# Matmul with rotary embedding: tiles in pairs of three PSUM banks, one VectorE multiply a pair, and every second tile transposed by VectorE blocks from four-piece loads

## The chip, the cores and the metric

One core of one Trainium2 chip. The metric is device microseconds (us) of one execution; lower is better. An execution more than 1.5% above the fastest of its kernel is called slow.

## The reference

```python
# x: 16 x 512 x 768 fp32, weight: 768 x 768 fp32, cos/sin: 512 x 64, 12 heads of 64
y = np.matmul(x, weight).reshape(batch, seq, n_heads, head_dim)
y1, y2 = y[..., :32], y[..., 32:]
out1 = y1 * cos1 - y2 * sin1
out2 = y2 * cos2 + y1 * sin2
out = np.concatenate([out1, out2], axis=-1).reshape(batch, seq, hidden)
```

There are 64 tiles of 128 rows. Both kernels cast each tile to fp16 and transpose it, so that the hidden dimension lies on the partitions, before they multiply it. In the kernel before that is 64 casts and, on TensorE, 384 transposes of 128 x 128, six a tile.

## The kernel before

A tile takes this way: a load of 384 KB on SyncE's queue; a cast to fp16 on ScalarE; six transposes on TensorE into `pt`, a copy out of PSUM on ScalarE; twelve matmuls into a two-bank PSUM tile `psy` (three such buffers); two multiplies on VectorE (by cos, and by the signed sin with the halves swapped); an add on GpSimd; a store on ScalarE's queue.

```python
    def load(i):
        xss[i] = xpool.tile([P, H], FP32, tag="xs", name="xs")
        nc.sync.dma_start(out=xss[i], in_=xv[i // SB, i % SB])
    ...
    def transpose(i, eng):
        xc = x16.pop(i)
        pt = pt_pool.tile([P, NKT, P], FP16, tag="pt", name="pt")
        for kt in range(NKT):
            nc.tensor.transpose(pt[:, kt, :], xc[:, ts(kt, P)], ident)
        xTT[i] = tpool.tile([P, NKT, P], FP16, tag="xT", name="xT")
        copy(eng, xTT[i], pt)
    ...
    def store(i):
        nc.scalar.dma_start(out=ov_dram[i // SB, i % SB], in_=ovs.pop(i))
    ...
    for i in range(FIRST, NMB):
        if i + AHEAD - FIRST < NMB:
            load(i + AHEAD - FIRST)
        if i + 1 < NMB:
            transpose(i + 1, nc.scalar)
        if 4 < i + 2 < NMB:
            cast(i + 2, nc.scalar)
        if i < NMB - 1:
            for kt in range(NKT):
                mm(i, kt)
            rope_whole(i)          # two multiplies on VectorE, one add on GpSimd
            store(i - 3)
```

## Time and profile before

| what | before |
|---|---|
| median of 3 runs (lowest to highest) | 166.97 us (166.83 to 168.94) |
| span of the profiled run, mean granted clock | 166.9 us, 0.983 |
| busy: TensorE, VectorE, GpSimd, ScalarE | 92%, 74%, 69%, 59% |

The table is read with the chain of waits in mind: TensorE is nearly full and is 88% of the chain, so a part counts if it shortens TensorE's stream and nothing else falls behind.

### The profile page before, as it was taken

How to read it: one execution, taken by the hardware profiler on the slowest of the kernel's cores; microseconds unless marked ns; L12 is line 12 of the kernel's file. 1: busy time of each engine (PE TensorE's matmuls, PEld its weight loads, DVE VectorE, ACT ScalarE, POOL GpSimd, SP SyncE). 2: the span in 40 equal slices, each digit the busy share in tenths (PEclk: the TensorE clock that was granted, in tenths of full speed). 3: DMA queues.
4: the chain of work that ended last, by engine and by line, in shares of the span. 5: the costliest groups of instructions: out<-in, count | busy, mean ns of one | idle time of the engine just before them, and what ended most of it. 6: DMA issues, size and time to landing. Idle time of an engine off the chain costs nothing.

```text
span 166.9 us, 3136 instructions
## 1 busy us (share of the span) xinstructions
PE 153.6 (92%) x1165; PEld 98.5 (59%) x1165; DVE 122.9 (74%) x142; ACT 97.9 (59%) x127; POOL 114.4 (69%) x67
## 2 busy tenths in 40 slices
PE   7657699999999999999999999999999999999930
PEld 2224466666666666666666666666666666666610
DVE  0522598777877688877778877778877778777792
ACT  3053366667766667766667766667666667666400
POOL 0000099777787777887777887777887777877770
PEclk9987999999999999999999999999999999999997
DMA  4999999999999999999999999999999984345544
GB/s 128 405 402 403 403 404 369 301 375 406 340 372 343 328 350 345 350 326 381 335 327 370 347 330 351 337 327 361 368 349 350 300 323 170 146 161 192 213 166 188
DMA packets 19887, 53.19 MB, mean 319 GB/s; under 512 B 2336, under 2 KB 2848, under 8 KB 19872
## 3 DMA queue, kind: packets, MB, share of 16 engines
q1 hardware_dynamic: 10368, 27.92, 49.5%
q10 hardware_dynamic: 9504, 25.07, 37.8%
q8 instruction: 9, 0.15, 0.5%
q14 instruction: 6, 0.05, 0.1%
HBM read 27.82 MB, written 25.17 MB: 317 GB/s over the span
## 4 chain that ended last, share of the span: by engine, by line
PE 88%; DMA 4%; ACT 2%; DVE 2%; issue 1%; SPq 1%; DVEq 0%
PE psy L103 74%; PE pt L93 13%; DMA xs<-in_x_dram 4%; PE psy L216 1%; DVE ov L130 1%; ACT xc L69 1%; ACT xT L69 1%; DVE qv L122 1%; SPq L80 1%; DVE tv L116 0%; SPq L75 0%; DVEq L130 0%; DVEq L116 0%
## 5 line engine op out<-in xcount | busy, mean ns | idle before, releaser
L130 POOL TENSOR_TENSOR ov<-tv,qv 128x768 f32<-128x768 f32 x63 | 114.2, 1816 | 47.4 <-DVE qv L122 46.2
L103 PE MATMUL psy<-w_sb,xT 128*128 128x512 f16 x756 | 135.1, 329 | 2.5 <-ACT xT L69 1.8
L103 PEld LDWEIGHTS <-xT 128*128 128x128 f16 x756 | 71.8, 99 | 44.9 <-ACT xT L69 2.1
L116 DVE TENSOR_TENSOR tv<-psy,cos_sb 128x768 f32<-128x768 f32 (+1 forms) x65 | 61.4, 944 | 31.7 <-PE psy L103 30.5
L69 ACT COPY xT<-pt 128x768 f16<-128x768 f16 x63 | 50.3, 798 | 51.2 <-PE pt L93 51.2
L122 DVE TENSOR_TENSOR qv<-psy,tee_sb 128x768 f32<-128x768 f32 (+1 forms) x65 | 60.7, 934 | 0.0
L69 ACT CAST xc<-xs 128x768 f16<-128x768 f32 x63 | 52.7, 836 | 5.8 <-DMA xs<-in_x_dram 5.8
L93 PE MATMUL pt<-ident,xc 128*128 128x128 f16 x384 | 31.9, 219 | 2.9 <-ACT xc L69 2.2
L93 PEld LDWEIGHTS <-xc 128*128 128x128 f16 x384 | 26.6, 98 | 12.3 <-ACT xc L69 3.0
L83 DVE CAST w_sb<-w_raw 128x768 f16<-128x768 f32 x6 | 3.3, 558 | 4.1 <-DMA w_raw<-in_weight_dram 4.1
L141 PE MATMUL cold_ps<-cold 128*128 128x512 f16 x13 | 4.6, 514 | 1.2 <-DVE cold L146 1.2
L141 PEld LDWEIGHTS <-cold 128*128 128x128 f16 x13 | 1.5, 126 | 3.3 <-issue 1.9
L71 DVE CAST xc<-xs 128x768 f16<-128x768 f32 x1 | 0.6, 560 | 3.7 <-DMA xs<-in_x_dram 3.7
L69 ACT ACT_TABLE_LOAD x1 | 1.3, 1283 | 2.1 <-issue 2.1
L216 PE MATMUL psy<-w_sb,xT 128*128 128x384 f16 x12 | 2.1, 326 | 0.0
L130 DVE TENSOR_TENSOR ov<-tv,qv 128x384 f32<-128x384 f32 x2 | 1.7, 862 | 0.1
L216 PEld LDWEIGHTS <-xT 128*128 128x128 f16 x12 | 1.2, 98 | 0.8
L71 DVE COPY xT<-pt 128x768 f16<-128x768 f16 x1 | 0.6, 556 | 0.6 <-PE pt L93 0.6
L146 DVE MEMSET cold<- 128x256 uint32 x1 | 0.3, 272 | 0.9 <-PEq L244 0.9
L244 POOL MEMSET const-float32-0.0<- 128x1 f32 x1 | 0.1, 98 | 0.2 <-issue 0.2
L185 DVE TENSOR_SCALAR tee_sb<-tee_sb 128x128 f32<-128x128 f32 x1 | 0.2, 220 | 0.0
L244 POOL MEMSET const-bfloat16-1.0<- 128x1 bf16 x1 | 0.1, 101 | 0.0
(2 smaller groups left out, 0.2 us busy)
## 6 DMA issues: line engine op xcount, KB each, us to landing
xs<-in_x_dram SPq DMA_DIRECT2D x64, 384.0 KB, 5.6
out_dram<-ov ACTq DMA_DIRECT2D x63, 384.0 KB, 4.8
w_raw<-in_weight_dram SPq DMA_DIRECT2D x6, 384.0 KB, 5.9
out_dram<-ov SPq DMA_DIRECT2D x2, 192.0 KB, 2.2
cos_sb<-in_cos_dram ACTq DMA_DIRECT2D x1, 128.0 KB, 5.2
tee_sb<-in_sin_dram ACTq DMA_DIRECT2D x1, 128.0 KB, 6.2
ident<-identity ACTq DMA_DIRECT2D x1, 32.0 KB, 3.6
```

The lines of the kernel that those rows point to most:

```text
L69: eng.copy(out=o, in_=i_)
L71: eng.tensor_copy(out=o, in_=i_)
L80: nc.sync.dma_start(out=w_raw[:, kt], in_=wv[:, kt])
L83: nc.vector.tensor_copy(out=w_sb[:, kt], in_=w_raw[:, kt])
L93: nc.tensor.transpose(pt[:, kt, :], xc[:, ts(kt, P)], ident)
L103: nc.tensor.matmul(psys[i][:, ds(noff, nsz)], xTT[i][:, kt, :], w_sb[:, kt, ds(noff % H, nsz)], start=(kt == 0), stop=(kt == NKT - 1),)
L116: nc.vector.tensor_tensor(out=tv.rearrange("p (h d) -> p h d", d=D), in0=ps.rearrange("p (h d) -> p h d", d=D), in1=cos_sb[:, sb, :].unsqu ...
L122: nc.vector.tensor_tensor(out=qv.rearrange("p (h t d) -> p h t d", t=2, d=HD), in0=ps.rearrange("p (h t d) -> p h t d", t=2, d=HD)[:, :, : ...
L130: add_eng.tensor_tensor(out=ov[:, ds(c0, n)], in0=tv, in1=qv, op=ADD)
L141: nc.tensor.matmul(cold_ps, cold[:, 0:P], cold, start=True, stop=True)
L146: nc.vector.memset(cold, 0.0)
L216: nc.tensor.matmul(psys[i][:, n, 0:sz], xTT[i][:, kt, :], w_sb[:, kt, ds(c0, sz)], start=(kt == 0), stop=(kt == NKT - 1),)
```

## The change

The intent is to take half of the transposes off TensorE. Tiles are handled in pairs, in a PSUM tile of three banks, so that one VectorE multiply (by cos and sin together, 3072 columns) and one GpSimd add (with the half swap, 1536 columns) serve a pair. From pair 3 on, the second tile of a pair is transposed by VectorE in blocks of 32 x 32. That completes a transpose only if the blocks lie in other places (with these tiles loaded whole, in experiment 1, the result has a relative error of 0.825). The load puts them there: four DMAs of 32 partitions each with runs of 768 B, two issued from SyncE and two from ScalarE. Pairs are also stored with one DMA instead of two, the loads at the start are reordered, and the last two pairs go tile by tile.

```diff
+    def by_blocks(n, s):
+        return n > 2 and s == 1
...
-    def load(i):
-        xss[i] = xpool.tile([P, H], FP32, tag="xs", name="xs")
-        nc.sync.dma_start(out=xss[i], in_=xv[i // SB, i % SB])
+    def load(n, s):
+        b, r = where(n, s)
+        xss[n, s] = xpool.tile([P, H], FP32, tag="xs", name="xs")
+        if by_blocks(n, s):
+            load_part(n, 0)
+            load_part(n, 1)
+        else:
+            nc.sync.dma_start(
+                out=xss[n, s], in_=x[b].rearrange("(p r) h -> r p h", r=SB)[r]
+            )
+
+    def load_part(n, q):
+        b, r = where(n, 1)
+        src = x[b].rearrange("(j a r) (q k) -> r q a j k", r=SB, a=R, q=NQ)   # R = 32, NQ = 4
+        dst = xss[n, 1].rearrange("p (j k) -> p j k", j=NQ)
+        eng = nc.sync if q < 2 else nc.scalar
+        eng.dma_start(out=dst[ts(q, R)], in_=src[r, q])
+
+    def load_rest(n):
+        if n < NP and by_blocks(n, 1):
+            load_part(n, 2)
+            load_part(n, 3)
...
+    def transpose_blocks(n, s):
+        xT = tpool.tile([P, NT, P, 2], FP16, tag="xT", name="xT")
+        nc.vector.transpose(
+            out=xT.bitcast(FP32).rearrange("p t m e -> p (t m e)"),
+            in_=x16.pop((n, s)).bitcast(FP32),
+        )
+        xTT[n, s] = xT.rearrange("p t m e -> p t e m")
...                                  # the loop over pairs
+        if n + 1 < NP and by_blocks(n + 1, 1):
+            transpose_blocks(n + 1, 1)
+        if n < NP - 1:
+            for c in CHUNKS:
+                mm(n, 0, *c)
...
+            prepare_b(n + 1, 0)      # ScalarE: copy of the transposed tile out of PSUM
+            prepare_a(n + 2, 0)      # ScalarE: cast
+            for c in CHUNKS:
+                mm(n, 1, *c)
...
+            prepare_a(n + 2, 1)      # ScalarE: cast
+            if n >= 3:
+                store(n - 3, nc.scalar)
+            load_rest(n + DEPTH - 2) # two more DMAs in ScalarE's stream
...
+                rope(n, 0, 2 * H, nc.gpsimd)
```

More of the change, by code (lines that the diff above doesn't have):

```diff
@@ L34, with where @@
     HD = D // 2
-    NKT = H // P
-    NMB = B * S // P
+    R = 32
+    NQ = P // R
+    NT = H // (2 * P)
     SB = S // P
-    NSPLIT = [(0, 512), (512, H - 512)]
-    HALVES = [(0, H // 2), (H // 2, H // 2)]
-    FIRST = 3
-    AHEAD = 8
-    xv = x.rearrange("b (p r) h -> b r p h", r=SB)
-    ov_dram = out.rearrange("b (p r) h -> b r p h", r=SB)
+    NP = B * SB // 2
+    CHUNKS = [(t, e) for t in range(NT) for e in range(2)]
+    DEPTH = 8
+    TAIL = 2
+    def where(n, s):
+        return 2 * (n // SB) + s, n % SB
+    def by_blocks(n, s):
+        return n > 2 and s == 1
     konst = ctx.enter_context(tc.tile_pool(name="konst", bufs=1))
     ident = konst.tile([P, P], FP16)
-    cos_sb = konst.tile([P, SB, D], FP32)
-    tee_sb = konst.tile([P, SB, D], FP32)
-    w_raw = konst.tile([P, NKT, H], FP32)
-    w_sb = konst.tile([P, NKT, H], FP16)
-    xpool = ctx.enter_context(tc.tile_pool(name="xpool", bufs=AHEAD + 3))
-    cpool = ctx.enter_context(tc.tile_pool(name="cpool", bufs=4))
-    tpool = ctx.enter_context(tc.tile_pool(name="tpool", bufs=FIRST + 2))
-    rpool = ctx.enter_context(tc.tile_pool(name="rpool", bufs=4))
-    opool = ctx.enter_context(tc.tile_pool(name="opool", bufs=5))
+    cold = konst.tile([P, 512], FP16)
+    sin_sb = konst.tile([P, SB, D], FP32)
+    csn = konst.tile([P, 2, SB, D], FP32)
+    w_raw = konst.tile([P, NT, 2, H], FP32)
+    w_sb = konst.tile([P, NT, 2, H], FP16)
+    xpool = ctx.enter_context(tc.tile_pool(name="xpool", bufs=2 * DEPTH + 2))
+    cpool = ctx.enter_context(tc.tile_pool(name="cpool", bufs=6))
+    tpool = ctx.enter_context(tc.tile_pool(name="tpool", bufs=7))
+    rpool = ctx.enter_context(tc.tile_pool(name="rpool", bufs=3))
+    opool = ctx.enter_context(tc.tile_pool(name="opool", bufs=4))
     pt_pool = ctx.enter_context(tc.tile_pool(name="pt", bufs=2, space=bass.MemoryType.PSUM))
-    py_pool = ctx.enter_context(tc.tile_pool(name="py", bufs=3, space=bass.MemoryType.PSUM))
-    cold = konst.tile([P, 512], FP16)
+    py_pool = ctx.enter_context(tc.tile_pool(name="py", bufs=2, space=bass.MemoryType.PSUM))
     cold_ps = pt_pool.tile([P, 512], FP32, tag="pt", name="cold_ps")
-    xss, x16, xTT, psys, ovs = {}, {}, {}, {}, {}
+    xss, x16, xTT, psys, tqs, ovs = {}, {}, {}, {}, {}, {}
     def copy(eng, o, i_):
@@ L71, in copy @@
             eng.tensor_copy(out=o, in_=i_)
-    def load(i):
-        xss[i] = xpool.tile([P, H], FP32, tag="xs", name="xs")
-        nc.sync.dma_start(out=xss[i], in_=xv[i // SB, i % SB])
-    wv = weight.rearrange("(kt p) n -> p kt n", p=P)
-    def load_w(kt):
-        nc.sync.dma_start(out=w_raw[:, kt], in_=wv[:, kt])
-    def cast_w(kt):
-        nc.vector.tensor_copy(out=w_sb[:, kt], in_=w_raw[:, kt])
-    def cast(i, eng):
-        x16[i] = cpool.tile([P, H], FP16, tag="xc", name="xc")
-        copy(eng, x16[i], xss.pop(i))
@@ L89, in transpose @@
-    def transpose(i, eng):
-        xc = x16.pop(i)
-        pt = pt_pool.tile([P, NKT, P], FP16, tag="pt", name="pt")
-        for kt in range(NKT):
-            nc.tensor.transpose(pt[:, kt, :], xc[:, ts(kt, P)], ident)
-        xTT[i] = tpool.tile([P, NKT, P], FP16, tag="xT", name="xT")
-        copy(eng, xTT[i], pt)
-    def mm(i, kt, parts=NSPLIT):
-        if i not in psys:
-            psys[i] = py_pool.tile([P, 2, 512], FP32, tag="psy", name="psy").rearrange(
+    def load(n, s):
[8 more added lines that the diff above has]
+            )
@@ new lines, in load_part, with load_w @@
+    def load_part(n, q):
[8 more added lines that the diff above has]
+            load_part(n, 3)
+    wv = weight.rearrange("(p t e) n -> t e p n", t=NT, e=2)
+    def load_w(t, e):
+        nc.sync.dma_start(out=w_raw[:, t, e], in_=wv[t, e])
@@ new lines, in cast_w, with cast, transpose @@
+    def cast_w(t, e):
+        nc.vector.tensor_copy(out=w_sb[:, t, e], in_=w_raw[:, t, e])
+    def cast(n, s, eng):
+        xc = cpool.tile([P, H], FP16, tag="xc", name="xc")
+        x16[n, s] = xc
+        src = xss.pop((n, s))
+        if by_blocks(n, s):
+            src = src.rearrange("p (j a t e) -> p t (j a) e", j=NQ, t=NT, e=2)
+        else:
+            src = src.rearrange("p (m t e) -> p t m e", t=NT, e=2)
+        copy(eng, xc.rearrange("p (t m e) -> p t m e", t=NT, e=2), src)
+    def transpose(n, s, eng):
+        xc = x16.pop((n, s)).rearrange("p (t m e) -> p t e m", t=NT, e=2)
+        pt = pt_pool.tile([P, NT, 2, P], FP16, tag="pt", name="pt")
+        for t, e in CHUNKS:
+            nc.tensor.transpose(pt[:, t, e, :], xc[:, t, e, :], ident)
+        xT = tpool.tile([P, NT, 2, P], FP16, tag="xT", name="xT")
+        copy(eng, xT, pt)
+        xTT[n, s] = xT
@@ new lines, in transpose_blocks, with alone, mm @@
+    def transpose_blocks(n, s):
[5 more added lines that the diff above has]
+        xTT[n, s] = xT.rearrange("p t m e -> p t e m")
+    def alone(n):
+        return n >= NP - 2
+    def mm(n, s, t, e, c0=0, c1=H):
+        key = (n, s) if alone(n) else n
+        base = 0 if alone(n) else s * H
+        if key not in psys:
+            psys[key] = py_pool.tile([P, 3, 512], FP32, tag="psy", name="psy").rearrange(
@@ L100, in mm @@
                 "p b n -> p (b n)"
             )
-        for noff, nsz in parts:
-            nc.tensor.matmul(
-                psys[i][:, ds(noff, nsz)],
-                xTT[i][:, kt, :],
-                w_sb[:, kt, ds(noff % H, nsz)],
-                start=(kt == 0),
-                stop=(kt == NKT - 1),
-            )
-    def rope(i, c0, n, ps, add_eng):
-        sb = i % SB
-        nh = n // D
-        tv = rpool.tile([P, H], FP32, tag="tv", name="tv")[:, :n]
-        qv = rpool.tile([P, H], FP32, tag="qv", name="qv")[:, :n]
+            if n < 2:
+                nc.tensor.matmul(
+                    psys[n][:, 512:1024], cold[:, 0:P], cold, start=True, stop=False
+                )
@@ new lines, in mm @@
+        cut = 256 if base else 512
+        for lo, hi in ((0, cut), (cut, H)):
+            lo, hi = max(lo, c0), min(hi, c1)
+            joined = n < 2 and 512 <= base + lo < 1024
+            if lo < hi:
+                nc.tensor.matmul(
+                    psys[key][:, ds(base + lo, hi - lo)],
+                    xTT[n, s][:, t, e, :],
+                    w_sb[:, t, e, ds(lo, hi - lo)],
+                    start=((t, e) == CHUNKS[0] and not joined),
+                    stop=((t, e) == CHUNKS[-1] and not (joined and s == 0)),
+                )
@@ L116, in rope @@
+    def rope(n, c0, c1, add_eng):
+        r = n % SB
+        w = c1 - c0
+        nh = w // D
+        if n not in tqs:
+            tqs[n] = rpool.tile([P, 2, 2 * H], FP32, tag="tq", name="tq")
+            ovs[n] = opool.tile([P, 2 * H], FP32, tag="ov", name="ov")
+        tq = tqs[n][:, :, ds(c0, w)]
+        ov = ovs[n][:, ds(c0, w)]
+        ps = psys[n, c0 // H][:, ds(c0 % H, w)] if alone(n) else psys[n][:, ds(c0, w)]
         nc.vector.tensor_tensor(
-            out=tv.rearrange("p (h d) -> p h d", d=D),
@@ L118, in rope @@
-            in0=ps.rearrange("p (h d) -> p h d", d=D),
-            in1=cos_sb[:, sb, :].unsqueeze(1).broadcast_to((P, nh, D)),
+            out=tq.rearrange("p j (h d) -> p j h d", d=D),
+            in0=ps.rearrange("p (h d) -> p h d", d=D)
+            .unsqueeze(1).broadcast_to((P, 2, nh, D)),
+            in1=csn[:, :, r, :].unsqueeze(2).broadcast_to((P, 2, nh, D)),
             op=MULT,
         )
-        nc.vector.tensor_tensor(
-            out=qv.rearrange("p (h t d) -> p h t d", t=2, d=HD),
-            in0=ps.rearrange("p (h t d) -> p h t d", t=2, d=HD)[:, :, ::-1, :],
-            in1=tee_sb[:, sb, :].rearrange("p (t d) -> p t d", t=2)
-            .unsqueeze(1).broadcast_to((P, nh, 2, HD)),
-            op=MULT,
-        )
@@ L129, in rope @@
-        ov = ovs[i]
-        add_eng.tensor_tensor(out=ov[:, ds(c0, n)], in0=tv, in1=qv, op=ADD)
-    def rope_whole(i):
-        ovs[i] = opool.tile([P, H], FP32, tag="ov", name="ov")
-        rope(i, 0, H, psys.pop(i)[:, 0:H], nc.gpsimd)
-    def store(i):
-        nc.scalar.dma_start(out=ov_dram[i // SB, i % SB], in_=ovs.pop(i))
-    def warm(n):
-        for _ in range(n):
+        add_eng.tensor_tensor(
+            out=ov.rearrange("p (h t d) -> p h t d", t=2, d=HD),
+            in0=tq[:, 0].rearrange("p (h t d) -> p h t d", t=2, d=HD),
+            in1=tq[:, 1].rearrange("p (h t d) -> p h t d", t=2, d=HD)[:, :, ::-1, :],
+            op=ADD,
+        )
@@ L141, in warm, with store @@
+    def store(n, eng, c0=0, c1=2 * H):
+        b, r = where(n, 0)
+        dst = out.rearrange("b (p r) h -> r p b h", r=SB)[r, :, b : b + 2]
+        src = ovs[n].rearrange("p (b h) -> p b h", b=2)
+        if c1 - c0 < 2 * H:
+            s = c0 // H
+            dst = dst[:, s, c0 - s * H : c1 - s * H]
+            src = src[:, s, c0 - s * H : c1 - s * H]
+        eng.dma_start(out=dst, in_=src)
+    def warm(k):
+        for _ in range(k):
             nc.tensor.matmul(cold_ps, cold[:, 0:P], cold, start=True, stop=True)
@@ L147 @@
     nc.scalar.dma_start(out=ident, in_=id_dram.ap())
-    load(0)
-    load_w(0)
-    load_w(1)
-    load(1)
-    nc.scalar.dma_start(out=cos_sb, in_=cos.rearrange("(p r) d -> p r d", r=SB))
-    nc.scalar.dma_start(out=tee_sb, in_=sin.rearrange("(p r) d -> p r d", r=SB))
-    load_w(2)
-    load_w(3)
-    load(2)
-    load_w(4)
-    load_w(5)
-    for i in range(FIRST, AHEAD):
-        load(i)
-    warm(9)
-    cast(0, nc.vector)
-    transpose(0, nc.vector)
-    warm(4)
-    for kt in (0, 1):
-        cast_w(kt)
-        mm(0, kt)
@@ L169 @@
-    cast(1, nc.scalar)
-    transpose(1, nc.scalar)
-    mm(1, 0)
-    mm(1, 1)
-    for kt in (2, 3):
-        cast_w(kt)
-        mm(0, kt)
-        mm(1, kt)
-    cast(2, nc.scalar)
-    transpose(2, nc.scalar)
-    for kt in range(4):
-        mm(2, kt)
-    cast_w(4)
-    for i in range(FIRST):
-        mm(i, 4)
-    cast_w(5)
+    for n in (0, 1):
+        for s in (0, 1):
+            load(n, s)
+    for t, e in CHUNKS:
+        load_w(t, e)
+    load(2, 0)
+    nc.sync.dma_start(out=csn[:, 0], in_=cos.rearrange("(p r) d -> p r d", r=SB))
@@ new lines, with prepare_a, prepare_b @@
+    nc.sync.dma_start(out=sin_sb, in_=sin.rearrange("(p r) d -> p r d", r=SB))
+    load(2, 1)
+    for n in range(3, DEPTH):
+        for s in (0, 1):
+            load(n, s)
+    def prepare_a(n, s):
+        if n < NP:
+            cast(n, s, nc.scalar)
+    def prepare_b(n, s):
+        if n < NP and not by_blocks(n, s):
+            transpose(n, s, nc.scalar)
+    warm(10)
+    cast(0, 0, nc.vector)
+    transpose(0, 0, nc.vector)
+    cast(0, 1, nc.scalar)
+    warm(4)
+    transpose(0, 1, nc.scalar)
@@ L185 @@
+    cast(1, 0, nc.vector)
+    warm(4)
+    transpose(1, 0, nc.vector)
+    cast(1, 1, nc.scalar)
+    warm(4)
+    transpose(1, 1, nc.scalar)
+    for k, c in enumerate(CHUNKS):
+        cast_w(*c)
+        mm(0, 0, *c)
+        mm(0, 1, *c)
+        if k > 0:
+            mm(1, 0, *CHUNKS[k - 1])
+    nc.vector.tensor_copy(out=csn[:, 1, :, 0:HD], in_=sin_sb[:, :, HD:D])
     nc.vector.tensor_scalar_mul(
-        out=tee_sb[:, :, 0:HD], in0=tee_sb[:, :, 0:HD], scalar1=-1.0
+        out=csn[:, 1, :, HD:D], in0=sin_sb[:, :, 0:HD], scalar1=-1.0
@@ L187 @@
     )
-    cast(3, nc.scalar)
-    mm(0, 5)
-    rope_whole(0)
-    mm(1, 5)
-    rope_whole(1)
-    transpose(3, nc.scalar)
-    cast(4, nc.scalar)
-    mm(2, 5)
-    rope_whole(2)
-    for i in range(FIRST, NMB):
-        if i + AHEAD - FIRST < NMB:
-            load(i + AHEAD - FIRST)
-        if i + 1 < NMB:
-            transpose(i + 1, nc.scalar)
-        if 4 < i + 2 < NMB:
-            cast(i + 2, nc.scalar)
-        if i < NMB - 1:
-            for kt in range(NKT):
-                mm(i, kt)
-            rope_whole(i)
-            store(i - 3)
@@ L210 @@
-    i = NMB - 1
-    ovs[i] = opool.tile([P, H], FP32, tag="ov", name="ov")
-    for n, (c0, sz) in enumerate(HALVES):
-        for kt in range(NKT):
-            if i not in psys:
-                psys[i] = py_pool.tile([P, 2, 512], FP32, tag="psy", name="psy")
-            nc.tensor.matmul(
-                psys[i][:, n, 0:sz],
-                xTT[i][:, kt, :],
-                w_sb[:, kt, ds(c0, sz)],
-                start=(kt == 0),
-                stop=(kt == NKT - 1),
-            )
-    for j in range(NMB - 4, NMB - 1):
-        store(j)
@@ L225 @@
-    for n, (c0, sz) in enumerate(HALVES):
-        rope(i, c0, sz, psys[i][:, n, 0:sz], nc.vector)
-        nc.sync.dma_start(out=ov_dram[i // SB, i % SB, :, ds(c0, sz)], in_=ovs[i][:, ds(c0, sz)])
+    rope(0, 0, 2 * H, nc.gpsimd)
+    prepare_a(2, 0)
+    load_rest(3)
+    load_rest(4)
+    prepare_a(2, 1)
+    mm(1, 0, *CHUNKS[-1])
+    prepare_b(2, 0)
+    for c in CHUNKS:
+        mm(1, 1, *c)
+    load_rest(5)
+    prepare_a(3, 0)
+    prepare_b(2, 1)
+    load_rest(6)
+    prepare_a(3, 1)
@@ new lines @@
+    load_rest(7)
+    rope(1, 0, 2 * H, nc.gpsimd)
+    for n in range(2, NP):
+        if n + DEPTH - 2 < NP:
+            for s in (0, 1):
+                load(n + DEPTH - 2, s)
+        if n + 1 < NP and by_blocks(n + 1, 1):
[3 more added lines that the diff above has]
+                mm(n, 0, *c)
+            if alone(n):
+                rope(n, 0, H, nc.gpsimd)
+            prepare_b(n + 1, 0)
+            prepare_a(n + 2, 0)
+            for c in CHUNKS:
+                mm(n, 1, *c)
+            prepare_b(n + 1, 1)
+            prepare_a(n + 2, 1)
+            if n >= 3:
+                store(n - 3, nc.scalar)
+            load_rest(n + DEPTH - 2)
+            if alone(n):
+                rope(n, H, 2 * H, nc.gpsimd)
+            else:
+                rope(n, 0, 2 * H, nc.gpsimd)
@@ L231 @@
+    n = NP - 1
+    for c in CHUNKS:
+        mm(n, 0, *c)
+    rope(n, 0, H, nc.gpsimd)
+    for c in CHUNKS:
+        mm(n, 1, *c, 0, 512)
+    for c in CHUNKS:
+        mm(n, 1, *c, 512, H)
+    store(n - 3, nc.scalar)
+    store(n - 2, nc.scalar)
+    store(n - 1, nc.sync)
+    store(n, nc.scalar, 0, H)
+    rope(n, H, H + 512, nc.vector)
+    store(n, nc.sync, H, H + 512)
+    rope(n, H + 512, 2 * H, nc.vector)
+    store(n, nc.scalar, H + 512, 2 * H)
 _INS = ['x', 'weight', 'cos', 'sin', 'n_heads']
```

## The prediction

> **What bounds the kernel now.** I read the page first: engines, slices, chain. Then the groups, the timeline of a stretch in the middle and of the end, the waits of the load queue, and last the packet records of the trace.
>
> ```profile
> PE 153.6 (92%) x1165; PEld 98.5 (59%) x1165; DVE 122.9 (74%) x142; ACT 97.9 (59%) x127; POOL 114.4 (69%) x67
> ...
> PE   7657699999999999999999999999999999999930
> ...
> PE 88%; DMA 4%; ACT 2%; DVE 2%; issue 1%; SPq 1%; DVEq 0%
> PE psy L103 74%; PE pt L93 13%; DMA xs<-in_x_dram 4%; PE psy L216 1%; DVE ov L130 1%; ACT xc L69 1%; ACT xT L69 1%; DVE qv L122 1%; SPq L80 1%; DVE tv L116 0%; SPq L75 0%; DVEq L130 0%; DVEq L116 0%
> ```
>
> PE is full from slice 6 to slice 37, and 87% of the chain is two of its lines: the matmuls into psy and the transposes into pt. Those 13% of transposes are what the change goes for. The timeline in the middle gives the period:
>
> ```profile
> 82.49 0.43 PEld L93 LDWEIGHTS <-xc 128*128 128x128 f16 x6
> 82.54 1.82 POOL L130 TENSOR_TENSOR ov<-tv,qv 128x768 f32<-128x768 f32 x1 [0.47 <-DVE qv L122]
> 82.60 0.50 PE L93 MATMUL pt<-ident,xc 128*128 128x128 f16 x6
> 82.87 0.96 DVE L116 TENSOR_TENSOR tv<-psy,cos_sb 128x768 f32<-128x768 f32 x1 [0.46 <-PE psy L103]
> 82.88 1.78 PEld L103 LDWEIGHTS <-xT 128*128 128x128 f16 x12
> 82.93 2.11 PE L103 MATMUL psy<-w_sb,xT 128*128 128x512 f16 x12
> ```
>
> The next tile's matmuls start at 85.22, so a tile takes 2.286 us (tile 4 starts at 23.47 on the weight loads, tile 62 at 156.00: 132.53 / 58 = 2.285). The chain in order of time gives 1.95 us for twelve matmuls. The rest, 0.335 us, is six transposes. VectorE, ScalarE and GpSimd each wait once a tile for something that PE set going. They are not the bound, but VectorE's idle share is only about 20%.
>
> The second thing to see is how near the DMA is to being one:
>
> ```profile
> DMA  4999999999999999999999999999999984345544
> GB/s 128 405 402 403 403 404 369 301 375 406 340 372 343 328 350 345 350 326 381 335 327 370 347 330 351 337 327 361 368 349 350 300 323 170 146 161 192 213 166 188
> ```
>
> ```profile
> SPq L75 <- ACT xc L69: 83.2, 47, 1.9
> ```
>
> The most it moves is 402 to 406 GB/s, in the early slices. Afterwards it moves about 344, which is what a 2.286 us tile asks for (2 x 393,216 bytes). The load queue waits for a buffer that ScalarE's cast frees, 47 times, so loads are ahead and PE sets the pace. Yet 344 of 405 is 85%: a pace 15% faster would meet the DMA.
>
> [...] The new stationary operands have a step of two. No instruction of this trace has one. [...]the same 128x384 add took 1.17 us beside GpSimd at the end, 0.56 us alone. [...]the typical packet of 256, 1024 and 3072 B took 18, 46 and 121 ns, about 9 ns plus 0.0366 ns per byte; 16 x 3072 B / 121 ns is 406 GB/s. [...]
>
> **The change part by part.**
> *Transposes.* From pair 3 on, one tile of two no longer goes through PE: the DMA brings in 32-row pieces so that 32x32 blocks complete the transpose. A pair then costs PE 2 x 1.95 + 0.335 = 4.235 us instead of 4.57. Over 29 pairs that is 9.7 us less, on the path.
>
> *VectorE.* Two multiplies of 768 and two again become one of 3072, plus one block transpose of 384 columns. From the groups:
>
> ```profile
> L116 DVE TENSOR_TENSOR tv<-psy,cos_sb 128x768 f32<-128x768 f32 x63 | 60.3, 957 | 31.6 <-PE psy L103 30.5 <-PE pt L93 0.9
> L116 DVE TENSOR_TENSOR tv<-psy,cos_sb 128x384 f32<-128x384 f32 x2 | 1.1, 550 | 0.1
> ```
>
> (957 - 550) / 384 is 1.06 ns a column, so 3072 columns take 0.957 + 2304 x 1.06 = 3.40 us. The transpose I estimate at the rate of the 384-column add, 0.56 us. Together 3.96, less some 0.1 of overlap: 3.9 of 4.235. It fits, with 0.3 us to spare. The three-bank product is given back about 3.5 us after its last matmul. With two such buffers PE needs it 4.235 us after, so no wait.
>
> *GpSimd.* One add of 1536 instead of two of 768: at most 2 x 1.816 = 3.63 of 4.235 us. It now does the half swap as well; I take that as free, as it is in VectorE's qv row (946 against 957 ns).
>
> *ScalarE.* Two casts and one copy out of PSUM, 2 x 0.84 + 0.80 = 2.47 us a pair, though the cast now gathers pairs. It also issues one store and two load pieces, at 0.33 us each or somewhat more, between. No bound.
>
> *Start.* The weights come after four x tiles; before, the last came after three, with cos and sin ahead. Bytes up to the last weight: 3.83 MB before, landed for its cast at 13.39; 3.97 MB now, so about 13.7. By then four tiles are transposed and three multiplied up to the last chunk. Cos and sin land at about 15.3; the first 3.40 us multiply can end at 19.2, and only then has PE a buffer for pair 2. PE ends pair 2 at 19.3 + 1.95 + 0.335 + 1.95 = 23.55. That is six tiles; in the kernel before, the seventh starts at 23.47 + 2 x 2.285 = 28.04. So 4.5 us less.
>
> *Middle.* Pairs 3 to 29: 27 x 4.235 = 114.3, to 137.9.
>
> *End.* The last two pairs are taken tile by tile, one three-bank buffer each. Counted from 137.9: pair 29's multiply ends at 3.5, the last block transpose at 4.0, the multiplies of 1536 columns (1.77 us) at 5.75, 7.5 and 9.65. PE waits for buffers about 3 us in all, and VectorE leads. Then a multiply of 1024 (to 10.85), an add of 512 columns, held by GpSimd's add until 12.0, a multiply of 512 and a short add (to 13.0). From the last add to the end of the span is now 166.9 - 163.97 = 2.9 us. End: 137.9 + 13.0 + 2.9 = 153.8 us.
>
> *DMA.* The block tiles come in packets of 768 B: 9 + 0.0366 x 768 = 37 ns, four for one of 121, so 148 for 121. Per pair: (384 x 121 + 512 x 37) / 16 = 4.09 us, with completions 4.1, against 4.235. That is 97% at the best rate seen. The 18 x buffers let loads run ahead before stores begin, so up to the end of pair 29 it has to do (41 plain loads and 27 pairs stored, 95 x 0.97 us, and 29 block tiles x 1.18) some 128 us of work by 137.9, having begun at about 2 and having to lead PE by a few. It fits only just. If the narrow pieces cost 3% to 8% of it, it doesn't, and each per cent past that is 1.3 us. I add 2 us for this: **156 us**.
>
> **Rivals.** *The DMA becomes the bound.* For it: the sum above[...]. If every block packet took double, 29 x 1.18 = 34 us more work, and the time would be near 180. Against it: the pieces go in two rings, one for each half of the partitions, and stores fill between them. With 10% lost I get some 161 us. It would show as ScalarE's cast waiting for xs through the middle. *VectorE becomes the bound.* If the block transpose takes 0.9 us or more instead of 0.56, its pair is over 4.235 and every 0.1 us costs 2.8 us. At 1.1 us: about 161. Its slope on such a form is in no row here. *The strided weight loads no longer hide.* A load takes 99 ns, and the 256-column matmul that hides it about as long (one third of 1.95 / 6 is 108). If a strided one took 150, six exposures a tile give 0.3 us back and the transposes' gain is gone: about 162. *GpSimd's swap is dear*: at over 4.235 us an add it sets the period; at 4.6, again over 160.
>
> **Range and chances.** Two bounds coincide near 154 and each rival only adds, so the range leans upward: 150 to 165. The lower end needs a shorter start or end than I count. Faster by over 2% (below 163.6): the middle would have to lose the whole 9.7 us and more for it to fail, since start and end give 3 or 4 us anyway: 0.87. Within 2%: 0.09. Slower: 0.04, nearly all the DMA.
>
> **What would show it.** Right: a PE pair of 4.2 to 4.3 us in the middle; VectorE rows of 3.4 and about 0.56 us; GpSimd's add at 3.4 to 3.65; casts still 0.84 us; weight loads of both kinds near 99 ns; PE past pair 2 at 23 to 24 us; 15 to 17 us after pair 29. Wrong: casts that wait for xs in the middle with the DMA at 9 throughout and under 370 GB/s (DMA rival); matmuls that wait on the multiply through psy (VectorE); matmuls longer on one tile of two (weight loads); multiplies waiting for tq (GpSimd).

## More of the kernel before

In the view of waits (engine and line, what it waited for: us in total, times, longest), ScalarE's copy out of PSUM waits only for the transposes that it copies:

```profile
ACT xT L69 <- PE pt L93: 51.2, 63, 2.8
```

The page's list of DMA issues gives the queue that issues, count, KB of each and median us from issue to landing:

```profile
xs<-in_x_dram SPq DMA_DIRECT2D x64, 384.0 KB, 5.6
out_dram<-ov ACTq DMA_DIRECT2D x63, 384.0 KB, 4.8
```

Two tiles take four DMAs: two loads on SyncE's queue, two stores on ScalarE's.

## The result and the profile after

The change is slower: 179.69 us (median of 4, 178.21 to 181.24, the last one slow) against 167.69 us (median of 4, 166.83 to 168.94). The ratio is 1.068, with a 95% interval of 1.054 to 1.082. (Ratios here are the mean time of one kernel's fast runs over that of the other's of the same rounds, so not quite the ratio of the medians quoted.) The profiled run: span 176.8 us, clock 0.992. The clock was no lower than in the profile of the kernel before (0.983), so it is not the cause.

The page of the kernel after, with slices of 4.4 us:

```profile
PE   7999774977837748889999799999999999997930
DMA  4999999999999999999999999999997664455866
GB/s 170 368 409 352 212 269 240 237 290 326 343 341 263 335 322 289 378 361 354 342 355 342 351 349 344 350 344 344 346 384 261 222 226 178 178 198 206 339 257 251
DMA 51%; PE 35%; DVE 4%; ACT 2%; ACTq 2%; SPq 2%; issue 1%; DVEq 0%
```

Counting slices from 0, TensorE has gaps in slices 4 to 17, 18 to 80 us. After that it is full but for slice 22, up to the end. The DMA shows 9 from slice 1 to 29, while it moves only 212 to 343 GB/s in slices 4 to 15, against 409 in slice 2. TensorE's share of the chain fell from 88% to 35%, the DMA's rose from 4% to 51%.

The groups, with different shapes kept apart (the mean of one is the number ahead of the second bar), are these:

```profile
L184 POOL TENSOR_TENSOR ov<-tq 128x1536 f32<-128x1536 f32 x30 | 103.7, 3457 | 62.7 <-DVE tq L177 45.4 <-DMA out_dram<-ov 16.1 <-DVE xT L131 1.2
L177 DVE TENSOR_TENSOR tq<-psy,csn 128x3072 f32<-128x3072 f32 x30 | 100.6, 3356 | 26.8 <-PE psy L159 26.7
L159 PEld LDWEIGHTS <-xT 128*128 128x128 f16 x768 | 72.5, 98 | 68.8 <-ACT xT L74 23.5 <-issue 1.5
L74 ACT CAST xc<-xs 128x768 f16<-128x768 f32 x62 | 53.0, 902 | 12.8 <-DMA xs<-in_x_dram 12.8
L131 DVE STREAM_TRANSPOSE xT<-xc 128x384 f32<-128x384 f32 x29 | 16.5, 570 | 5.7 <-ACT xc L74 5.7
```

No instruction became dear: a weight load takes 98 ns (99 before), a copy out of PSUM 800 (798), a cast 902 (836). What changed is what they wait for:

```profile
ACT xT L74 <- DMA xs<-in_x_dram: 38.4, 15, 4.7
...
PEld L159 <- ACT xT L74: 23.5, 18, 3.4
...
ACT xc L74 <- DMA xs<-in_x_dram: 12.8, 5, 3.9
```

The first line is odd and is the key. `xT L74` on ScalarE is the copy of a finished transpose *out of PSUM*. It doesn't read xs. Yet it waited 38.4 us for landings of x, three times as long as the casts, which do read xs. The second line passes it on: TensorE's weight loads wait for that copy. The timeline shows how a copy comes to wait for a load (start, duration, what, and in brackets the idle time before with its releaser):

```profile
50.20 0.85 ACTq L95 DMA_DIRECT2D xs<-in_x_dram  x2
...
51.14 0.80 ACT L74 COPY xT<-pt 128x768 f16<-128x768 f16 x1 [4.68 <-DMA xs<-in_x_dram]
...
52.00 2.12 PE L159 MATMUL psy<-w_sb,xT 128*128 128x512 f16 x12 [2.67 <-ACT xT L74]
```

ScalarE's two load issues stand ahead of the copy in its stream. They did not go before 50.20, and the copy, and with it TensorE, stood behind them. What they waited for is in the trace's records of landings. All 194 DMAs of this kernel, of both queues, report their landing on eight semaphores. The issues around 50 us, each with the DMA before it on the same semaphore (us):

| issue | at | the DMA before it on its semaphore | issued at | landed at |
|---|---|---|---|---|
| load, SyncE L95 | 49.67 | load, SyncE L85 | 41.93 | 49.47 |
| load, SyncE L85 | 50.19 | load, ScalarE L95 | 42.41 | 50.00 |
| load, ScalarE L95 | 50.20 | load, SyncE L95 | 42.73 | 50.17 |
| load, SyncE L95 | 50.66 | load, ScalarE L95 | 43.06 | 50.51 |
| load, ScalarE L95 | 50.70 | load, SyncE L95 | 44.14 | 50.67 |

Each of these predecessors is the eighth issue before. ScalarE's two issues began 0.02 us after the landings. It is so in the whole trace: each of the 186 issues that have a predecessor on their semaphore began after its landing, and 102 of them, 52 on ScalarE, within 0.09 us. In the kernel before it is 130 of 130, but only 14 within 0.09 us and none on ScalarE. In the kernel after the predecessor is the sixth to tenth issue before, on the mean the eighth, and never were more than eight DMAs in flight, in either kernel. We call these semaphores slots below: in these traces a DMA is not issued until its slot's last one, about the eighth before it, has landed. The chain in order of time (start us, duration us, what) shows it as landing after landing, each setting off the next issue, until 75 us:

```profile
22.35 5.71 DMA xs<-in_x_dram
28.43 6.39 DMA xs<-in_x_dram
34.89 6.69 DMA out_dram<-ov
41.66 7.59 DMA out_dram<-ov
...
69.12 6.16 DMA xs<-in_x_dram
75.72 0.81 ACT xT L74
76.57 2.12 PE psy L159 x12
```

Before, two tiles took four DMAs, so eight DMAs spread over two pairs of tiles: 8 / 4 x 4.57 = 9.1 us, against 5.6 us from issue to landing. Now a pair takes six, three of them from ScalarE, and at full pace eight spread over 8 / 6 x 4.235 = 5.6 us. The page's list of issues has landings of about that:

```profile
out_dram<-ov ACTq DMA_DIRECT2D x30, 768.0 KB, 5.9
xs<-in_x_dram SPq DMA_DIRECT2D x35, 384.0 KB, 6.0
xs<-in_x_dram SPq DMA_DIRECT2D x58, 96.0 KB, 4.9
xs<-in_x_dram ACTq DMA_DIRECT2D x58, 96.0 KB, 4.7
```

That made a theory, with rivals to be told apart. **A, order and number:** six DMAs a pair over eight slots, three of them standing in ScalarE's stream ahead of its copies. **B, narrowness:** the packets of a DMA that lands on 32 partitions are slow. The kernel before has no such DMA, so the prediction reckoned from wide ones. **C, small packets:** 768 B instead of 3072 B. The packet records of the trace spoke for B: a 768 B packet took 48.5 to 49.0 ns on the mean, where the prediction reckoned 37. The expectations call A theory waits, B theory ports and C theory small packets; ports is a name only, since no run shows what makes narrow packets slow.

### The profile page after: what moved, and what is told of

It is laid out like the page before. It is cut to its first block, busy times and chain, and to the rows that moved or that the text cites.

```text
span 176.8 us, 2628 instructions
## 1 busy us (share of the span) xinstructions
PE 148.2 (84%) x1002; PEld 88.6 (50%) x1002; DVE 131.1 (74%) x79; ACT 77.5 (44%) x96; POOL 109.2 (62%) x37
## 4 chain that ended last, share of the span: by engine, by line
DMA 51%; PE 35%; DVE 4%; ACT 2%; ACTq 2%; SPq 2%; issue 1%; DVEq 0%
DMA xs<-in_x_dram 43%; PE psy L159 33%; DMA out_dram<-ov 8%; DVE tq L177 3%; PE pt L124 2%; SPq L95 1%; DVE ov L184 1%; ACT xc L74 1%; ACT xT L74 1%; ACTq L95 1%; ACTq L199 1%; SPq L85 0%; ACTq L74 0%; DVEq L177 0%
## 5 line engine op out<-in xcount | busy, mean ns | idle before, releaser
L159 PE MATMUL psy<-w_sb,xT 128*128 128x512 f16 (+1 forms) x768 | 132.8, 326 | 18.5 <-ACT xT L74 17.1
L184 POOL TENSOR_TENSOR ov<-tq 128x1536 f32<-128x1536 f32 (+1 forms) x33 | 109.0, 3307 | 62.7 <-DVE tq L177 45.4
L177 DVE TENSOR_TENSOR tq<-psy,csn 128x3072 f32<-128x3072 f32 (+3 forms) x35 | 107.7, 3080 | 27.4 <-PE psy L159 27.1
L74 ACT CAST xc<-xs 128x768 f16<-128x768 f32 x62 | 53.0, 902 | 12.8 <-DMA xs<-in_x_dram 12.8
L74 ACT COPY xT<-pt 128x768 f16<-128x768 f16 x33 | 26.4, 800 | 71.6 <-DMA xs<-in_x_dram 38.4
L131 DVE STREAM_TRANSPOSE xT<-xc 128x384 f32<-128x384 f32 x29 | 16.5, 570 | 5.7 <-ACT xc L74 5.7
L124 PE MATMUL pt<-ident,xc 128*128 128x128 f16 x210 | 17.8, 222 | 1.6 <-ACT xc L74 1.5
L124 PEld LDWEIGHTS <-xc 128*128 128x128 f16 x210 | 14.8, 99 | 7.6 <-ACT xc L74 2.3
L203 PE MATMUL cold_ps<-cold 128*128 128x512 f16 x22 | 7.8, 508 | 1.2 <-DVE cold L208 1.2
L203 PEld LDWEIGHTS <-cold 128*128 128x128 f16 x22 | 2.6, 126 | 4.3 <-issue 2.5
L184 DVE TENSOR_TENSOR ov<-tq 128x512 f32<-128x512 f32 (+1 forms) x2 | 2.3, 1144 | 0.1
L151 PEld LDWEIGHTS <-cold 128*128 128x128 f16 x2 | 0.2, 98 | 0.0
```

Source lines behind the costliest of these rows:

```text
L74: eng.copy(out=o, in_=i_)
L124: nc.tensor.transpose(pt[:, t, e, :], xc[:, t, e, :], ident)
L131: nc.vector.transpose(out=xT.bitcast(FP32).rearrange("p t m e -> p (t m e)"), in_=x16.pop((n, s)).bitcast(FP32),)
L151: nc.tensor.matmul(psys[n][:, 512:1024], cold[:, 0:P], cold, start=True, stop=False)
L159: nc.tensor.matmul(psys[key][:, ds(base + lo, hi - lo)], xTT[n, s][:, t, e, :], w_sb[:, t, e, ds(lo, hi - lo)], start=((t, e) == CHUNKS[0] ...
L177: nc.vector.tensor_tensor(out=tq.rearrange("p j (h d) -> p j h d", d=D), in0=ps.rearrange("p (h d) -> p h d", d=D) .unsqueeze(1).broadcast ...
```

## The experiments

Edits are against the kernel after, except those of 8 and 10 (against 7), 9 (against 5), 11 and 14 (against 10), 12 (against 9) and 13 (against 4). Several give wrong results: the block transpose wants the pieces' layout, and they load other bytes. That changes no instruction's size. Times are medians; kernels ran with runs of the kernel before (168.24 us beside the first four, 166.82 beside the next four, 166.94 beside the next three, 168.36 beside the last three). So the kernel before differed by 1.5 us between calls, and a difference of medians from two calls is uncertain by about as much.

**1. The block tile in one whole load** (wrong). It takes B, C and A away at once and keeps the rest of the change.

```diff
-        if by_blocks(n, s):
-            load_part(n, 0)
-            load_part(n, 1)
+        if False:
+            pass
         else:
             nc.sync.dma_start(
...                                  # load_rest does nothing
```

> Every second tile still goes through the block transpose, but comes in as one load of 128 partitions and 3072 B rows on the load queue (the results of these tiles are wrong on purpose). This takes away all that is special about the loads: narrow pieces, 768 B packets, six DMAs a pair instead of three, and loads on ScalarE's queue. All theories of the loads: 153 to 157 us, the sum of my prediction without the DMA term, pairs every 4.24 us from pair 3 on and no ScalarE copy behind a DMA. If it stays above 170, the loss is not in the loads but in the pairs or in the block transpose.

Measured: 157.17 us, ratio 0.935 (0.928 to 0.943), span 155.6 us. The page and the waits of this run:

```profile
PE   6999899999999999999999999999999999996900
GB/s 142 374 397 400 401 401 400 405 416 411 415 410 416 416 409 415 410 415 416 409 416 415 414 412 416 417 413 330 178 168 175 206 202 202 204 202 214 337 243 223
```

```profile
ACT xT L74 <- PE pt L121: 52.8, 30, 2.2
```

TensorE is full, and ScalarE's copy waits only for the transposes that it copies. The whole 22 us lie in how the block tiles are loaded. The rest of the change works.

**2. Four pieces on the same two queues, but 128 partitions wide** (768 B packets; wrong). It takes B away and keeps A and C.

```diff
-        src = x[b].rearrange("(j a r) (q k) -> r q a j k", r=SB, a=R, q=NQ)
-        dst = xss[n, 1].rearrange("p (j k) -> p j k", j=NQ)
+        src = x[b].rearrange("(p r) (q k) -> r q p k", r=SB, q=NQ)
+        dst = xss[n, 1].rearrange("p (q k) -> p q k", q=NQ)
-        eng.dma_start(out=dst[ts(q, R)], in_=src[r, q])
+        eng.dma_start(out=dst[:, q], in_=src[r, q])
```

> The same four DMAs of 96 KB on the same two queues with the same 768 B packets, but each over all 128 partitions (wrong results on purpose). Only the narrowness goes. Theory ports ([...]packets stretch): 768 B packets back at about 37 ns, and 156 to 163 us. Theory waits (each DMA waits for the landing of the eighth before it, and ScalarE stands behind such a wait): the number of DMAs is unchanged, so ScalarE's copies go on waiting for loads, 172 to 180 us. Theory small packets: 172 to 180 us too.

Measured: 171.28 us, ratio 1.021 (1.012 to 1.029). Packets of 768 B took 37.6 to 37.7 ns, as predicted. Still 14 of the 22 us remain. The copies out of PSUM go on waiting for landings, less than the 38.4 us of the change:

```profile
ACT xT L74 <- DMA xs<-in_x_dram: 26.2, 10, 7.3
```

The time is lost early: from 24 to 50 us TensorE was busy for 18.4 of 26 us, from 57 to 135 us for 77.6 of 78. The granted clock was 0.82 in that early stretch (0.956 in the whole run), and TensorE's busy time a matmul was 180 ns there against 142 from 57 to 135 us, so a part of this loss goes with the lower clock; the other three runs, at 0.965 to 0.976, were no faster. Narrowness is not enough to explain the result.

**3. Narrow pieces of whole rows** (32 partitions, 3072 B packets; wrong). It takes C away and keeps A and B.

```diff
-        src = x[b].rearrange("(j a r) (q k) -> r q a j k", r=SB, a=R, q=NQ)
-        dst = xss[n, 1].rearrange("p (j k) -> p j k", j=NQ)
+        src = x[b].rearrange("(q a r) h -> r q a h", r=SB, a=R)
-        eng.dma_start(out=dst[ts(q, R)], in_=src[r, q])
+        eng.dma_start(out=xss[n, 1][ts(q, R)], in_=src[r, q])
```

> Four DMAs of 32 partitions on the same two queues, each of whole 3072 B rows (wrong results on purpose). Only the 768 B packets go. Theory ports and theory waits: 172 to 180 us, as now. Theory small packets: 156 to 163 us.

Measured: 177.39 us, ratio 1.057 (1.048 to 1.066), against 1.068 for the change. The difference is 2 us and the intervals overlap, so small packets (C) are worth little beside A and B; these runs don't tell it from nothing.

**4. All four pieces from SyncE's queue** (right). It takes the pieces out of ScalarE's stream and leaves its stores there.

```diff
-            load_part(n, 0)
-            load_part(n, 1)
+            for q in range(NQ):
+                load_part(n, q)
...                                  # load_rest does nothing
-        eng = nc.sync if q < 2 else nc.scalar
+        eng = nc.sync
```

> The four narrow pieces with their 768 B packets, all on the load queue, none on ScalarE's (results right). ScalarE no longer stands behind the landing of a load. Theory waits: its copies stop waiting for xs, PE gets its operands, 157 to 166 us. Theory ports: no better[...]: 175 to 190 us with under 300 GB/s in the first third.

Measured: 174.59 us, ratio 1.041 (1.034 to 1.048). The stall changes its place. Pairs run at 4.235 us up to 53.6 us, then at 5.0 us on average (20 pairs in 99.2 us), and now it is the casts that wait:

```profile
ACT xc L74 <- DMA xs<-in_x_dram: 52.6, 35, 3.8
```

Loads come too late as such. That is what the prediction's DMA rival would look like, but it mixes A and B still, so both had to be measured alone.

**5. One whole load, and three loads of 16 B a partition in the pieces' places** (wrong): the number and the places of the DMAs, without the narrowness and without the bytes.

```diff
+        src = x[b].rearrange("(p r) h -> r p h", r=SB)[r]
+        if q == 0:
+            nc.sync.dma_start(out=xss[n, 1], in_=src)
+        else:
+            eng = nc.sync if q < 2 else nc.scalar
+            eng.dma_start(out=tiny[:, n, q], in_=src[:, 0:4])
```

> The kernel of the whole-tile run (157 us) with three loads of 16 B per partition added for each block tile, one on the load queue and two on ScalarE's, just where the pieces stood (wrong results on purpose). [...]only the number of DMAs a pair goes back to six, with two of them in ScalarE's queue. Theory waits: 166 to 174 us, with ScalarE's copies behind DMA landings before 60 us. Theories ports and small packets: 157 to 159 us.

Measured: 175.24 us, ratio 1.054 (1.044 to 1.064), 18 us above experiment 1. The three small loads carry 0.18 MB in all, and their packets took 9 ns. The waits of this run:

```profile
ACT xT L75 <- DMA tiny<-in_x_dram: 15.8, 8, 3.6
ACT xT L75 <- POOL ov L187: 15.8, 4, 4.7
```

The copy out of PSUM, which reads neither, waits for the small loads' landings and for GpSimd's sum, that is, for the slots of the loads and for the data of the store that stand ahead of it in ScalarE's stream. A is shown, and it suffices to bring back most of the loss. Its price is no fixed number: experiment 2 has as many DMAs in the same places and lost 14 us. Why it lost less is open.

**6. No block tiles** (right): every tile transposed on TensorE, the rest of the change kept.

```diff
     def by_blocks(n, s):
-        return n > 2 and s == 1
+        return False
```

> All tiles are transposed by TensorE again and loaded whole (results right); pairs, the one multiply a pair, the start and the end stay. Three DMAs a pair. By the sums of the prediction 29 x 0.335 = 9.7 us more than the whole-tile run: 166 to 168 us, about the kernel before. Pairs of 4.57 us on TensorE.

Measured: 167.63 us, ratio 1.006 (1.002 to 1.009). Against experiment 1, the block transposes are worth 10.5 us for 29 tiles, 0.36 us a tile. The other parts of the change together gain nothing.

**7. Block tiles together, in every second pair, in four pieces of two tiles, all from SyncE** (right): 3.5 DMAs a pair with nearly the same narrow bytes (30 block tiles).

```diff
-        return n > 2 and s == 1
+        return n > 2 and n % 2 == 1
...
+            src = x[b : b + 2].rearrange("b (j a r) (q k) -> r q a (b j) k", r=SB, a=R, q=NQ)
+            dst = xs.rearrange("p b (j k) -> p (b j) k", j=NQ)
+            for q in range(NQ):
+                nc.sync.dma_start(out=dst[ts(q, R)], in_=src[r, q])
+        elif n > 2:                  # a plain pair: one load for both tiles
```

> The block tiles are put together in every second pair (both of its tiles by blocks, none in the next), so that one narrow piece carries the same 32 partitions of two tiles in 16 KB more rows: four DMAs for two block tiles, one load for two plain tiles, two stores, so 3.5 DMAs a pair instead of six, all loads on the load queue (results right). Packets and narrowness are unchanged. Theory waits: 156 to 163 us. Theory ports as the main cause: 170 us or more, with VectorE and TensorE waiting for casts that wait for xs.

Measured: 171.96 us with one of four runs slow, ratio 1.027 (1.016 to 1.038). The expectation was missed. With few DMAs it is still slower than before, and its casts wait for data:

```profile
ACT xc L74 <- DMA xs<-in_x_dram: 28.4, 14, 3.6
```

**8. The same with pieces 128 partitions wide** (wrong). It separates what is left of B from A at 3.5 DMAs a pair.

```diff
-            src = x[b : b + 2].rearrange("b (j a r) (q k) -> r q a (b j) k", r=SB, a=R, q=NQ)
-            dst = xs.rearrange("p b (j k) -> p (b j) k", j=NQ)
+            src = x[b : b + 2].rearrange("b (p r) (q k) -> r q p b k", r=SB, q=NQ)
+            dst = xs.rearrange("p b (q k) -> q p b k", q=NQ)
...
-                nc.sync.dma_start(out=dst[ts(q, R)], in_=src[r, q])
+                nc.sync.dma_start(out=dst[q], in_=src[r, q])
```

> As the alternate run, but each of the four DMAs covers all 128 partitions with 768 B packets (wrong results on purpose). Theory waits: within 2 us of the alternate run. Theory ports: clearly faster than it, near 157 us, by what narrowness costs at this number of DMAs.

Measured: 162.15 us, ratio 0.972 (0.969 to 0.974), 9.8 us below experiment 7 with the same number, size and order of DMAs. The 768 B packets took 37.6 ns here and 51.7 ns there. The windows view of 76 to 135 us (length, busy time of TensorE matmuls, TensorE weight loads, VectorE, ScalarE and GpSimd, granted clock, DMA share, GB/s), for experiment 7 and then for experiment 8:

```profile
76.00:135.00 59.00, 54.09 (x376) 33.42 (x375) 47.88 (x25) 31.20 (x39) 43.34 (x13) 1.00 1.05 335
```

```profile
76.00:135.00 59.00, 59.00 (x421) 37.40 (x420) 53.33 (x29) 33.51 (x43) 50.37 (x16) 1.00 0.85 324
```

In experiment 7 the DMA engines have no free time (a share of 1.05) and move 335 GB/s, in experiment 8 they move about as much in 0.85 of their time. (The share sums the time of packets, so it can pass 1. A full share alone doesn't show a bound: experiment 1 has 1.03 from 24 to 76 us, at 410 to 413 GB/s, with TensorE full.) So B is shown too, apart from A: the same bytes of x in packets of the same size, and only the partitions on which they land differ. Why the partitions matter is not shown. Experiment 8 is still 5 us above experiment 1; its casts waited 19.6 us for x, and what makes that was not tested.

**9. Experiment 5 with the small loads all from SyncE** (wrong); ScalarE issues only its stores.

```diff
-            eng = nc.sync if q < 2 else nc.scalar
-            eng.dma_start(out=tiny[:, n, q], in_=src[:, 0:4])
+            nc.sync.dma_start(out=tiny[:, n, q], in_=src[:, 0:4])
```

> As the run with the three tiny loads (175 us), but all three of them on the load queue, none on ScalarE's (wrong results on purpose). Tells the two halves of the wait theory apart. If the loss is ScalarE standing in its queue behind another DMA's landing: 157 to 161 us. If it is the chain of eighth-before landings by itself, wherever the DMAs are issued: 168 to 175 us.

Measured: 171.13 us, but two of four runs were slow; the fast ones were 168.00 and 169.85, ratio 1.011 (1.001 to 1.020). The profile fell in a slow run, so only its waits are used, not its sizes: the copies out of PSUM waited for landings of x (12.4 us), of the small loads (9.9) and of the stores (5.2), though the stores are the only DMAs that ScalarE issues in this loop. Inconclusive by itself; experiment 12 finishes it.

**10. Block tiles in every fourth pair only** (right): 16 tiles instead of 30, otherwise experiment 7.

```diff
-        return n > 2 and n % 2 == 1
+        return n % 4 == 3
```

> The alternate kernel with block tiles only in every fourth pair, so 16 instead of 30 tiles (results right). Half of the narrow traffic, 2.75 DMAs a pair. From the run without blocks (167.6 us) 16 x 0.36 us of TensorE work less, 0.36 being what the whole-tile run gained a tile over it: 161.9 us if the loads keep up; 165 to 168 if narrowness still holds them up.

Measured: 163.96 us, ratio 0.982 (0.977 to 0.987). TensorE is full from about 30 us on.

**11. As 10, but every second pair after pair 16** (right), on the thought that late loads have had time to run ahead.

```diff
-        return n % 4 == 3
+        return (n % 4 == 3 or n > 16 and n % 2 == 1)
```

> As the quarter run, with block tiles in every second pair from pair 17 on, 24 tiles in all (results right). 167.6 - 24 x 0.36 = 159.0 us if the loads keep up in the second half, where the buffers start full; above 163 if the narrow loads cannot.

Measured: 165.07 us; of four runs two were slow, the fast ones 163.20 and 164.30; ratio 0.980 (0.972 to 0.987). The expectation was missed: eight more block tiles bring nothing over experiment 10.

**12. Experiment 9 with the stores of the loop moved to SyncE** (wrong): six DMAs a pair as in the change, none of them in ScalarE's stream.

```diff
-                store(n - 3, nc.scalar)
+                store(n - 3, nc.sync)
```

> The run with the tiny loads on the load queue (168 to 171 us), with the stores of the loop on the load queue too, so that ScalarE issues no DMA between its copies (wrong results on purpose). Six DMAs a pair and each behind the landing of the eighth before it, as there. In that run ScalarE's copies still waited 27 us for DMA landings, through the stores in its queue, and no cast waited for data. If standing in ScalarE's queue is how the chain of landings reaches TensorE: 157 to 160 us. If the chain delays the data or the stores themselves: 165 us or more.

Measured: 161.48 us, ratio 0.963 (0.956 to 0.970), 13.8 us below experiment 5, at the same number of DMAs. The copy waits for its transposes again, in the waits of this run:

```profile
ACT xT L75 <- PE pt L124: 55.9, 32, 1.9
...
POOL ov L184 <- DMA out_dram<-ov: 20.9, 19, 3.8
```

So ScalarE's place behind its own issues is the route by which the number of DMAs reaches TensorE. What is left over experiment 1, 4 us, comes after pair 29 (20.6 us from its multiply to the end, against 17.1), where stores come late and GpSimd waits for output buffers.

**13. The change itself with all its loop's DMAs on SyncE** (right): experiment 4 and the stores too.

```diff
-        eng = nc.sync if q < 2 else nc.scalar
+        eng = nc.sync
...
-                store(n - 3, nc.scalar)
+                store(n - 3, nc.sync)
```

> The changed kernel with all its narrow pieces and all stores of the loop on the load queue (results right): ScalarE issues nothing between its copies. What is left is narrowness, small packets and late data. If the narrow loads are a bound of their own: 168 us or more, casts that wait for xs, 768 B packets near 45 ns. If not: under 163 us.

Measured: 170.47 us, ratio 1.014 (1.005 to 1.024). With A's route closed, 13 us over experiment 1 remain, and 9 us over experiment 12, which has as many DMAs on the same queue and no narrow pieces: that is what narrowness and small packets cost here. The 768 B packets took 52.6 ns. The windows view of 50 to 76 us, then the waits:

```profile
50.00:76.00 26.00, 24.33 (x172) 14.95 (x170) 21.41 (x11) 12.87 (x17) 18.47 (x7) 1.00 1.06 336
```

```profile
POOL ov L182 <- DMA out_dram<-ov: 33.6, 23, 6.6
...
DVE tq L175 <- POOL ov L182: 19.1, 23, 1.5
...
ACT xc L74 <- DMA xs<-in_x_dram: 8.8, 6, 4.2
```

The casts were expected to do the waiting and did so for 8.8 us only. The full DMA hits through late stores: GpSimd finds no free output buffer, VectorE no free `tq`. So a full DMA needn't show as casts that wait: in experiment 4 they did so for 52.6 us, here for 8.8.

**14. Experiment 10 with the stores on SyncE** (right).

```diff
-                store(n - 3, nc.scalar)
+                store(n - 3, nc.sync)
```

> The quarter run (164.0 us, results right) with the stores of the loop on the load queue. There ScalarE's copies waited for almost no DMA, so I expect within 1.5 us of it, 162.5 to 165.5; it is tried as the best candidate against both kernels.

Measured: 163.93 us, ratio 0.978 (0.971 to 0.984), the same as experiment 10. Of the versions that compute the right result, 10 and 14 are the best, with 11 not told apart from them: about 2% under the kernel before and 9% under the change.

## Why the prediction was wrong

The predicted 156.0 us (150 to 165) was missed by 24 us. Its steps, one by one:

- **Transposes and TensorE's pair: right.** In the kernel after, pairs start every 4.235 us where nothing stalls them (134.46, 138.69, 142.93 us). The blocks are worth 10.5 us (experiments 1 and 6), predicted 9.7.
- **VectorE and GpSimd: right.** 3.36 and 0.57 us against 3.40 and 0.56; 3.46 us against at most 3.63, with the swap free.
- **Strided weight loads: right.** 98 ns for the operands of the new stride, as for the others.
- **Start and middle: right once loads are whole.** In experiment 1 pair 2's multiply starts at 24.05 us (predicted end of its matmuls 23.55), and 27 pairs later at 138.56, 4.241 us each.
- **End: mis-sized by 1.2 us.** From there to the end 17.1 us against 15.9; the 512-column add on VectorE took 1.86 us, as in the kernel after, where for 1.31 us of it GpSimd's adds ran beside it. (In the kernel before, an add of 384 columns took 1.17 us beside GpSimd and 0.56 alone.) So "start and end give 3 or 4 us anyway" was too much: start and end together gave 2.3 us at most in experiment 1 (the span fell by 11.3, the middle from pair 3 to 29 by 27 x 0.335 = 9.0), and nothing in experiment 6.
- **The sum without the DMA: right to 1%.** 153.8 us predicted, 155.6 us the span of experiment 1.
- **ScalarE: the step that failed.** "It also issues one store and two load pieces, at 0.33 us each or somewhat more, between. No bound." The time of the issues was counted, not what they wait for. Each waited for the landing of its slot's last DMA, about the eighth before it (52 of ScalarE's issues began within 0.09 us of that landing), ScalarE's copies stood behind it, and TensorE behind the copies: 38.4 us of waits of this kind in the kernel after. Number and place alone cost 18 us (experiment 5 against 1), of which 14 go if ScalarE issues none (experiment 12). (The casts, which now gather pairs, took 0.90 us for a predicted 0.84 and did no harm in experiment 1; the two on VectorE at the start took 0.95, against 0.56 for the one of the kernel before.)
- **DMA: the second step that failed.** It took 37 ns for a block packet from wide packets and added 2 us. Measured: 48.5 to 49.0 ns in the kernel after, 45.3 to 52.6 in experiments 4, 7, 10 and 13. "Against it: the pieces go in two rings, one for each half of the partitions" showed no gain: from SyncE alone they took 45.3 and 52.6 (experiments 4 and 13). The 121 ns for a wide packet was the typical one; the mean of the loads was 144.7 ns already in the kernel before, 149.4 after and 123.6 in experiment 1. "If the narrow pieces cost 3% to 8% of it, it doesn't" fit was the right worry, at a wrong size: the packets cost 1.2 to 1.4 times as much and slow others beside them (wide loads of 146.8 ns in experiment 7, 129.2 in 8). Narrowness was worth 8 us (change against experiment 2) and 10 us (7 against 8), with small packets 9 us (13 against 12). Small packets as such: about 2 us, within the noise.
- **The rivals.** "The DMA becomes the bound" came half true, but its sign, casts waiting for xs, carried 12.8 us against 38.4 us of the copies. That its "near 180" is the measured time is luck: it took packets of double the time, where the runs show 1.2 to 1.4 times, and nothing waiting in ScalarE's stream. A list of rivals that holds no "an issue waits in a compute engine's stream" can't name it.

The two causes don't add: A alone brings back 18 of the 22 us (experiment 5 against 1), narrowness 8 to 10, together more than the 22. Both make landings late against the eight slots, which may be why, but no run shows it. What of the 22 us in the kernel after belongs to which can't be said. It is also open why the stall in the kernel after ends by itself near 76 us.

## What to carry to other kernels

Count the DMAs of a period and ask from whose stream each is issued, not only how many bytes they bring: divide the most DMAs that the trace shows in flight (eight here) by the number per period, and compare that time with issue to landing. Keep issues that may have to wait out of the stream of an engine on the critical path's way (13.8 us here, experiment 5 against 12); a wait of an instruction for something it doesn't read is the sign that one stands ahead of it. And before taking a packet's duration from wide DMAs for narrow ones, measure one (48.5 to 49.0 ns here, where 37 was reckoned).
